# A two-layer decoder trunk on one core: every large tile at a multiple of 512 bytes with the weights' tiles 256 bytes further on, a different start, and copies of q by DMA

## The chip, the cores and the metric

The kernel runs on one core of one Trainium2 chip. The metric is the device time of one execution in microseconds (us). Before the change it is 2411.27 us, the median of three runs (2409.95 to 2413.39). Two times within about 0.2% of each other (4.8 us) can't be told apart by a measurement of this kernel.

The core has a matrix engine (TensorE; in the rows PE for its matmuls and PEld for its loads of the stationary operand), a vector engine (VectorE, DVE), a scalar engine (ScalarE, ACT), GpSimd (POOL), and a queue engine (SyncE, SP) that issues most DMAs. Each runs its own list of instructions in order, and semaphores join them.

## The reference

Input x is (1, 512, 1024) in float32: 512 positions, width 1024. Two layers follow, and a final RMSNorm. A layer is:

```python
h = rms_norm(x, norm_mix_g[i])
proj = h @ w_in[i]          # q_r,k_r,v_r,g_r | q_n,kv_n,gate_n | m_a,m_b
...
o_r = retention(qr, kr, vr)                      # 4 heads, dk 256, dv 512, rotary q and k
y_ret = (silu(g_r) * group_norm(o_r)) @ w_o_ret[i]
o_n = nsa(q_n, k_c, v_c, k_s, v_s, k_w, v_w, ...)  # 16 heads of 64, 2 key groups
y_nsa = o_n @ w_o_nsa[i]
x = x + (sigmoid(m_a) * y_ret + sigmoid(m_b) * y_nsa) @ w_out[i]
h = rms_norm(x, norm_ffn_g[i])
a, b = split(h @ w_ffn_in[i]);  x = x + (silu(a) * b) @ w_ffn_out[i]   # hidden 2816
```

The sparse attention (nsa) has three branches per head: compressed keys and values (an MLP with gelu over overlapping blocks of 32 positions, for keys and for values), selected blocks, and a window. With 512 positions all blocks are selected and the window covers everything, so the last two are full causal softmax attentions with different keys. A T5 relative bias is added to all three.

## The kernel before

**Precision and matmuls.** Every product is made of three fp32r matmuls. An operand is split into a rounded part (hi) and the rest (lo): `split` (L78) makes hi with a copy on ACT and lo with a subtraction on DVE. `mm3` (L119) then adds hi by hi, hi by lo and lo by hi into one PSUM bank (L122, L123, L124). A matmul streams its moving operand, up to 512 columns, past a stationary operand of 128 by 128 that PEld loads; the load of the next one runs while the present one streams. In the rows, `f<-hh,wh` names the output bank, the moving and the stationary operand.

**Weights.** `raw` (L86) loads up to 1 MB of a weight into a tile wr (three buffers) by one DMA on SP. `cut` (L94) splits a part of it into wh and wl (three buffers each). SP issues a load when its buffer is free, which is when the wl of an earlier user has been made.

**Two kinds of projection.** In `proj_t` (L126) the weights are stationary and the activations (hh and hl, 512 columns) move. In `proj_n` (L717), and in the values of the attention, the weights move and slices of the activations are stationary.

**Addresses.** A tile's place in SBUF follows from the sizes of all tiles allocated ahead of it, each rounded to 32 bytes: first the constants (cols, ident, rb, kcz, ...), then pool sb with the 37 slots "u" of 2 KB, ks, p, pt, gate, cv, strip, mt, ld, then the small tiles (sm), then the weights' pool wp. Before the change the slots u and the tiles p, pt and ks lie at 416 bytes past a multiple of 512, cv and strip at 160, and wr, wh and wl at 96. All slices that matmuls of 512 columns read begin at steps of 512 bytes in these tiles.

**The start.** `setup` (L133) loads constants and clears kcz. `start_x` (L232) loads x transposed in eight tiles xt (256 KB each) and the first weights, those of the compressed keys and values (1 MB), in the order two xt, the weights, six xt. `make_h` (L198) scales each xt by the norm's gain and splits it into hh and hl. The norm's other factor, rstd per position, comes later: `acc_sq` (L203) squares each xt on ACT and adds on POOL, `norm_stats` (L211) sums over partitions with small matmuls (L216) and takes the power -1/2 on POOL (L220), and `norm_bcast` (L222) spreads it: a copy rep on DVE (L225), four transposes (L229), and the tile rb on ACT (L230), by which projections are then multiplied.

**Keys and values of the attention.** `nsa_kv` (L261) makes, in this order: the two projections psc for compression (48 matmuls), the norm's sums, the key projection psk[0], rb, psk[1]. Then it steps through generators that others share: `compress` for k and v (L324; z and xa on DVE, hi and lo of xa into p or pt tiles, 32 matmuls of 256 columns at L362 in two halves, a gelu, a small projection) and `nsa_q` (L411; a projection of 24 matmuls per half quad, then qd, hi and lo, and copies of both to the other 64 partitions at L431). `keys(br)` (L272) makes the key tiles ks on DVE and ACT. The order of these steps is

```python
next(comp["k"]); fill(9)
next(comp["k"]); next(comp["k"]); next(comp["v"])
keys(0); fill(9)
next(comp["v"]); next(comp["v"]); keys(1)
```

where `fill(9)` is half a quad of q. Then come the values (96 matmuls of 304 columns), and after that 16 heads of attention, merged with the next quads' q and with gate projections.

**Who sets the order.** A scheduler puts each engine's instructions in order by the program's order and by when it expects them to be ready. `issue_after` adds an edge, so that what a block traces on one engine comes behind a given instruction there.

Of the kernel before, what the change touches and what calls it, by code (L numbers as in the profile page):

```python
# [8 lines left out]
F32 = mybir.dt.float32  # L9
F32R = mybir.dt.float32r  # L10
AF = mybir.ActivationFunctionType
ALU = mybir.AluOpType
AX = mybir.AxisListType

P = 128
T = 512
D = 1024
NT = T // P
KD = D // P
# [3 lines left out]
HN = 16  # L23
# [8 lines left out]
class Builder:  # L32
# [86 lines left out]
    def mm3(self, ps, items, start=True, stop=True):  # L119
        n = len(items)  # L120
        for i, (lh, ll, rh, rl) in enumerate(items):
            self.nc.tensor.matmul(ps, lh, rh, start=start and i == 0, stop=False)  # L122
            self.nc.tensor.matmul(ps, lh, rl, start=False, stop=False)  # L123
            self.nc.tensor.matmul(ps, ll, rh, start=False, stop=stop and i == n - 1)  # L124

    def proj_t(self, w, j, acts, bank=None):  # L126

# [5 lines left out]
    def setup(self):  # L133
        nc, a = self.nc, self.a
        self.bv = self.dr.tile([HN, 640], F32, tag="bv", name="bv")
        self.cols = self.const("cols", [P, 104])
        nc.sync.dma_start(self.cols, a["c_cols"])
        self.gmix = [self.cols[:, l * 8 : l * 8 + 8] for l in range(DEPTH)]
        self.gffn = [self.cols[:, 16 + l * 8 : 24 + l * 8] for l in range(DEPTH)]
        self.pos = {"k": [self.cols[:, 40 + l * 16 : 56 + l * 16] for l in range(DEPTH)],  # L140
                    "v": [self.cols[:, 72 + l * 16 : 88 + l * 16] for l in range(DEPTH)]}
        self.ident = self.const("ident", [P, P])
        nc.gpsimd.dma_start(self.ident, a["c_ident"])
        self.setup_bias()
        self.mhalf = self.const("mhalf", [P, NT])
        nc.vector.memset(self.mhalf, -0.5)
        self.ones = self.const("ones", [P, 1])
        nc.vector.memset(self.ones, 1.0)
        self.rb = self.const("rb", [P, T])
        self.rstd = self.const("rstd", [P, NT])  # L150
        self.hrstd = self.const("hrstd", [P, NT])
        self.kcz = [self.const(f"kcz{g}", [P, 224], F32R) for g in range(2)]
        for g in range(2):
            nc.vector.memset(self.kcz[g].bitcast(F32), 0.0)
        self.xs = self.dr.tile([KD, P, T], F32, tag="xs", name="xs")
        self.gs = self.dr.tile([2 * KD, P, T], F32, tag="gs", name="gs")
        self.gr = self.dr.tile([4 * NSPILL, P, T], F32, tag="gr", name="gr")
        self.ys = self.dr.tile([KD, P, T], F32, tag="ys", name="ys")
        self.cmask = self.const("cmask", [P, NT, 32])
        nc.gpsimd.dma_start(self.cmask, a["c_cmask"].rearrange("p (i n) -> p i n", n=32))  # L160
# [71 lines left out]
    def start_x(self):  # L232

        nc = self.nc
        xts = [self.u("xt") for _ in range(KD)]
        w = self.a["w_in"][0][:, C_KV : C_KV + 256].rearrange("(k p) n -> p k n", p=P)
        for k in range(2):
            last = nc.sync.dma_start(xts[k], self.a["c_xt"][k])
        with self.tc.issue_after(last.ins):
            raw = self.raw([(lambda v: v, w)], KD, 256)  # L240
        with self.tc.issue_after(self.last_load.ins):
            for k in range(2, KD):
                self.last_x = nc.sync.dma_start(xts[k], self.a["c_xt"][k])
        h = [self.make_h(xts[k], self.gmix[0][:, k : k + 1]) for k in range(2)]
        with self.tc.issue_after(self.last_hi.ins):
            self.first_w = [self.cut(raw[:, :, j * P : (j + 1) * P]) for j in range(2)]
        h += [self.make_h(xts[k], self.gmix[0][:, k : k + 1]) for k in range(2, KD)]
        self.first_h = self.last_hi

        def stats():  # L250
            self.bias_rows()
            acc = None
            for xt in xts:
                acc = self.acc_sq(acc, xt)
            self.norm_stats(acc)

        self.stats = stats, self.norm_bcast
        return h


    def nsa_kv(self, l, h, q0):  # L261
        nc, w = self.nc, self.a["w_in"][l]
        view = lambda c, n, k0=0, kt=KD: w[k0 * P : (k0 + kt) * P, c : c + n].rearrange("(k p) n -> p k n", p=P)
        wc = self.first_w if l == 0 else self.wcols(w, 0, KD, C_KV, 256)
        psc = [self.proj_t(wc, j, h, "f") for j in range(2)]
        with self.tc.issue_after(self.last_x.ins) if l == 0 else nullcontext():
            wk = self.raw([(lambda v: v[:, :, :P], view(C_KV + 256, P)), (lambda v: v[:, :, P:], view(C_KV + 512, P))], KD, 256)
        self.stats[0]()
        nc.vector.tensor_scalar(self.hrstd, self.rstd, 0.5, None, ALU.mult)
        ks = [self.sb.tile([P, 2, T], F32R, tag=f"ks{g}", name=self.nm("ks"), bufs=1) for g in range(2)]  # L270

        def keys(br):  # L272
            kd, kh = self.u("kd"), self.u("kh", F32R)
            nc.vector.tensor_tensor(kd, psk[br], self.rb, ALU.mult)
            lo, hi = slice(0, 64), slice(64, P)
            self.split(ks[0][lo, br], ks[0][hi, br], kd[lo])
            self.split(kh[hi], ks[1][hi, br], kd[hi])
            nc.scalar.activation(ks[1][lo, br], kd[hi], AF.Copy)

        def values(half):  # L280
            return self.chunk([(lambda v: v[:, :, 0:P], view(C_KV + 384, P, half * 4, 4)),
                               (lambda v: v[:, :, P : 256 + 48], view(C_KV + 640, P + 48, half * 4, 4))], 4, 304, "k")

        with self.tc.issue_after(self.first_h.ins) if l == 0 else nullcontext():
            wk = [self.cut(wk[:, :, br * P : (br + 1) * P]) for br in range(2)]
        psk = [self.proj_t(wk, 0, h, "a")]
        self.stats[1]()
        psk.append(self.proj_t(wk, 1, h, "a"))
        comp = {kind: self.compress(l, kind, psc[i]) for i, kind in enumerate("kv")}
        fill = lambda n: [next(q0, None) for _ in range(n)]  # L290
        next(comp["k"])
        fill(9)
        next(comp["k"])
        next(comp["k"])
        next(comp["v"])
        keys(0)
        fill(9)
        next(comp["v"])
        next(comp["v"])
        keys(1)  # L300
        vs = [self.sb.tile([P, 4, 2, 64], F32R, tag="u", name=self.nm("vs")) for _ in range(NT)]
        gate = self.sb.tile([P, NT, HN, 3], F32, tag="gate", name=self.nm("gate"), bufs=1)
        pss = [self.bank(b) for b in "aaoo"]
        for half in range(2):
            wv = values(half)
            for t in range(NT):
                ts = slice(t * P, (t + 1) * P)
                self.mm3(pss[t][:, :304], [(h[half * 4 + k][0][:, ts], h[half * 4 + k][1][:, ts], wv[k][0], wv[k][1])
                                           for k in range(4)], start=half == 0, stop=half == 1)
            if half == 0:  # L310
                for kind in "kv":
                    next(comp[kind], None)
        for t in range(NT):
            src = pss[t][:, :256].rearrange("p (b d) -> p b d", d=64)
            rc = self.rstd[:, t : t + 1]
            nc.scalar.activation(vs[t][:, :, 0, :], src, AF.Copy, scale=rc)
            nc.vector.scalar_tensor_tensor(vs[t][:, :, 1, :], src, rc, vs[t][:, :, 0, :].bitcast(F32), ALU.mult, ALU.subtract)
            gt = gate[:, t].rearrange("p h b -> p (h b)")
            nc.scalar.activation(gt, pss[t][:, 256:304], AF.Tanh, scale=self.hrstd[:, t : t + 1])
            nc.vector.tensor_scalar(gt, gt, 0.5, 0.5, ALU.mult, ALU.add)  # L320
        return ks, vs, gate
# [88 lines left out]
    def nsa_q(self, l, h, quad, qs):  # L410
# [7 lines left out]
        for a in range(2):  # L418
# [7 lines left out]
            for g in range(2):  # L426
# [1 line left out]
                r, o = (slice(x * 64, x * 64 + 64) for x in (g, 1 - g))  # L428
                self.split(hi[r], lo[r], d[r])
                for x in (hi, lo):  # L430
                    nc.scalar.activation(x[o], x[r].bitcast(F32), AF.Copy)  # L431
                qs.append((hi, lo))
            yield

# [468 lines left out]
    def last_ffn(self, l, x, h):  # L903
# [3 lines left out]
        for hf in range(2):  # L907
            gf.append(self.tile("p", NPB))
            nc.sync.dma_start(gf[hf], self.a["norm_final_g"][None, hf * 512 : hf * 512 + 512].broadcast_to([P, 512]))
        ss = self.small("ss", 2 * NT)  # L910
        base = self.small("base", NT)
        for k0, kt in GROUPS:
            hid = self.hidden(l, h, k0, kt)
# [59 lines left out]
WR = 3  # L973
WH = 3
# [4 lines left out]
AT = {"scores": (0, 0.5), "values": (0, 0.8), "finish": (0.6, 0.6), "fill": (0.1, 0.7)}  # L979
QAT = (2, 2)  # L980
NSPILL = 3
FILL = [20, 18, 8, 8, 14, 14, 8, 8, 14, 14, 8, 8, 14, 14, 14, 14, 14, 12]
BANKS = {"a": 2, "o": 2, "t": 2, "f": 2}
CYCLE = "afo"
# [65 lines left out]
```

## Time and profile before

| | |
|---|---|
| median of 3 runs | 2411.27 us |
| the profiled execution, its own time | 2411.87 us |
| its span, first to last instruction | 2409.8 us |
| granted TensorE clock, mean | 0.996 |
| PE busy | 2364.8 us (98%), 11042 matmuls |
| PEld busy | 1936.3 us (80%) |
| DVE, ACT, POOL busy | 1386.1, 1070.7, 258.2 us |
| DMA | 260 MB, mean 108 GB/s |

Busy time of PE is no measure of its speed: matmuls overlap, and the end of each is modelled, so a matmul that shows 0.39 us starts 0.23 us behind the one ahead. Where matmuls follow each other without a wait, the distance of their starts is their cost; it is read from a count in a window, or from the starts in the timeline. A wait is put down to what released it last.

### The profile page before, as it was taken

The page shows a single profiled execution, that of the slowest core. Times are in us where ns is not written, and L with a number is a line of the kernel's source. Part 1 is how long each engine was busy: PE and PEld are TensorE (multiplying, and loading weights), DVE is VectorE, ACT ScalarE, POOL GpSimd, SP SyncE. Part 2 cuts the span into 40 slices and gives each one's busy share as a digit, 9 for nine tenths or more (in the row PEclk, how much of TensorE's full clock was granted, in tenths as well). Part 3 has the DMA queues.
Part 4 walks back from the last instruction along what each step waited for, and adds up shares of the span by engine and source line. Part 5 has one row for each costly group of instructions (what it writes and reads, how often), then busy time and mean ns, then how long its engine had stood idle before and what let it go on. Part 6 is the DMA issues. An engine that isn't in the chain of part 4 may idle for free.

```text
span 2409.8 us, 29134 instructions
## 1 busy us (share of the span) xinstructions
PE 2364.8 (98%) x11042; PEld 1936.3 (80%) x11042; DVE 1386.1 (58%) x2715; ACT 1070.7 (44%) x1926; POOL 258.2 (11%) x224
## 2 busy tenths in 40 slices
PE   7999999999999999999989999999999999999998
PEld 5887778888887888888878777788888878888887
DVE  6777887354574633333577877864555754434344
ACT  5677786233333422222356777742433343322222
POOL 3000000010030110110200000001100202101010
PEclk9999999999999999999999999999999999999999
DMA  7532223522342522323444232244232533223221
GB/s 210 143 89 74 74 83 93 183 75 95 106 159 86 163 88 91 101 90 98 142 142 129 81 84 70 78 130 147 92 92 92 179 107 130 89 87 105 88 96 61
DMA packets 234172, 260.35 MB, mean 108 GB/s; under 512 B 42214, under 2 KB 178438, under 8 KB 234033
## 3 DMA queue, kind: packets, MB, share of 16 engines
q1 hardware_dynamic: 220688, 236.93, 32.3%
q10 hardware_dynamic: 13152, 21.37, 2.4%
q8 instruction: 86, 1.41, 0.2%
q14 instruction: 54, 0.43, 0.1%
q0 software_dynamic: 192, 0.21, 0.0%
HBM read 235.36 MB, written 23.11 MB: 107 GB/s over the span
## 4 chain that ended last, share of the span: by engine, by line
PE 90%; ACT 4%; DVE 4%; issue 1%; POOL 1%; DMA 0%; SPq 0%; ACTq 0%; POOLq 0%
PE f L122 12%; PE f L123 12%; PE f L124 12%; PE a L123 8%; PE a L122 8%; PE o L122 8%; PE o L123 8%; PE o L124 8%; PE a L124 8%; PE t L564 2%; PE o L556 1%; PE o L557 1%; ACT wh L79 1%; PE a L529 1%; PE a L530 1%
## 5 line engine op out<-in xcount | busy, mean ns | idle before, releaser
L79 ACT ACTIVATE wh<-wr 128x1024 fp32r<-128x1024 f32 (+3 forms) x406 | 397.9, 980 | 952.9 <-PE f L123 227.5
L80 DVE TENSOR_TENSOR wl<-wr,wh 128x1024 fp32r<-128x1024 f32 (+3 forms) x406 | 465.7, 1151 | 227.2 <-ACT wh L79 224.9
L122 PE MATMUL f<-hh,wh 128*128 128x512 f32 x936 | 373.1, 399 | 3.2 <-ACT wh L79 3.2
L123 PE MATMUL f<-hl,wh 128*128 128x512 f32 x936 | 369.9, 395 | 0.0
L124 PE MATMUL f<-hh,wl 128*128 128x512 f32 x936 | 368.1, 394 | 1.2 <-DVE wl L80 1.1
L124 PEld LDWEIGHTS f<-hh,wl 128*128 128x128 f32 x936 | 176.4, 188 | 41.9 <-DVE wl L80 3.6
L122 PEld LDWEIGHTS f<-hh,wh 128*128 128x128 f32 x936 | 176.4, 188 | 37.7 <-ACT wh L79 5.0
L123 PEld LDWEIGHTS f<-hl,wh 128*128 128x128 f32 x936 | 176.6, 189 | 30.7
L511 ACT ACTIVATE p<-p,nmx 128x512 f32<-128x512 f32 (+3 forms) x256 | 142.5, 557 | 53.7 <-DVE nmx L510 51.2
L80 DVE TENSOR_TENSOR pt<-t,pt 128x512 fp32r<-128x512 f32 (+3 forms) x256 | 123.2, 484 | 50.6 <-ACT pt L79 49.3
L874 POOL TENSOR_TENSOR fa<-fa,rb 128x512 f32<-128x512 f32 x44 | 77.6, 1763 | 562.2 <-ACT fa L873 562.2
L510 DVE CUSTOM_DVE_ANT_0 p<-a,strip 128x512 f32<-128x512 f32 (+3 forms) x256 | 119.4, 483 | 25.2 <-PE a L530 15.6
L123 PE MATMUL a<-hl,wh 128*128 128x512 f32 x336 | 132.4, 394 | 0.0
L122 PE MATMUL a<-hh,wh 128*128 128x512 f32 x336 | 132.4, 394 | 0.0
L124 PE MATMUL a<-hh,wl 128*128 128x512 f32 x336 | 131.2, 390 | 0.0
L79 ACT ACTIVATE pt<-t 128x512 fp32r<-128x512 f32 (+3 forms) x256 | 109.1, 427 | 47.6 <-PE t L564 43.5
L123 PE MATMUL o<-hl,wh 128*128 128x512 f32 x328 | 129.2, 394 | 0.0
L122 PE MATMUL o<-hh,wh 128*128 128x512 f32 x328 | 129.0, 393 | 0.0
L124 PE MATMUL o<-hh,wl 128*128 128x512 f32 x328 | 127.9, 390 | 0.0
L564 PE MATMUL t<-ident,p 128*128 128x128 f32 x640 | 113.9, 273 | 0.0
L564 PEld LDWEIGHTS t<-ident,p 128*128 128x128 f32 x640 | 81.2, 140 | 23.6 <-DVE pt L80 1.7
L556 PE MATMUL o<-pt,vs 128*128 128x512 f32 (+3 forms) x256 | 92.8, 365 | 3.2 <-ACT pt L79 3.2
(405 smaller groups left out, 4842.7 us busy)
## 6 DMA issues: line engine op xcount, KB each, us to landing
wr<-in_w_in SPq DMA_DIRECT2D x66, 1024.0 KB, 5.3
wr<-in_w_ffn_in SPq DMA_DIRECT2D x44, 1024.0 KB, 5.1
wr<-in_w_ffn_out SPq DMA_DIRECT2D x18, 1024.0 KB, 5.0
wr<-in_w_o_ret SPq DMA_DIRECT2D x16, 1024.0 KB, 5.0
wr<-in_w_in SPq DMA_DIRECT2D x36, 256.0 KB, 4.6
strip<-bv SPq DMA_DIRECT2D x32, 256.0 KB, 4.0
gs<-mt ACTq DMA_DIRECT2D x32, 256.0 KB, 2.0
wr<-in_w_o_nsa SPq DMA_DIRECT2D x16, 512.0 KB, 6.5
```

The lines of the kernel that those rows point to most:

```text
L79: self.nc.scalar.activation(hi, src, AF.Copy)
L80: (eng or self.nc.vector).tensor_sub(lo, src, hi.bitcast(F32))
L122: self.nc.tensor.matmul(ps, lh, rh, start=start and i == 0, stop=False)
L123: self.nc.tensor.matmul(ps, lh, rl, start=False, stop=False)
L124: self.nc.tensor.matmul(ps, ll, rh, start=False, stop=stop and i == n - 1)
L510: nc.vector.tensor_tensor_reduce(p, src, self.backwards(strip, w - 1, w), -1.0, BIG, ALU.add, ALU.min, nmx[:, c])
L511: nc.scalar.activation(p, p, AF.Exp, scale=-1.0, bias=nmx[:, c], accum_out=sm[:, c])
L529: nc.tensor.matmul(ps[:, :w], qh[:, ts], ks[:, br, :w], start=True, stop=False)
L530: nc.tensor.matmul(ps[:, :w], ql[:, ts], ks[:, br, :w], start=False, stop=True)
L556: nc.tensor.matmul(po[:, j * P :], lhs, th, start=br == 0 and j == 0, stop=False)
L564: nc.tensor.transpose(pt[:, (i - j) * P : (i - j + 1) * P], pr[br][i][:, j * P : (j + 1) * P], self.ident)
L874: nc.gpsimd.tensor_mul(t, t, self.rb)
```

## The change

- Two unused tiles, pad in the constants (96 bytes) and pad among the small tiles (448 bytes), gate widened from 192 to 256 columns, and ss with two buffers instead of six. With these the slots u, p, pt, ks, cv and strip begin at multiples of 512 bytes, and wr, wh and wl 256 bytes past one.
- In setup an activation on hrstd, and 32 matmuls of 224 columns on the cleared kcz, whose result nobody reads.
- `start_x` loads weights in four pieces of 256 KB, each ahead of a pair of xt, and cuts and splits them pair by pair. The first two projections go through k in the outer loop and through the two columns of tiles in the inner one.
- In layer 0 the squares are added on DVE instead of POOL, the sums come behind psk[0] and rb behind the first half of psk[1]; `bias_rows` comes after the statistics. In layer 1 the sums come between the two psc and rb behind them. hrstd is made behind all of that.
- The first step of the values' compression comes ahead of the third of the keys', and keys(0) comes behind the values' last matmuls.
- The copies at L431 (64 of 64 by 512) become DMAs issued on SP.

```diff
-            self.nc.tensor.matmul(ps, ll, rh, start=False, stop=stop and i == n - 1)
+            self.last_mm = self.nc.tensor.matmul(ps, ll, rh, start=False, stop=stop and i == n - 1)
...
+        self.const("pad", [P, 24])
...
+        self.small("pad", PAD, bufs=1)
...
+        nc.scalar.activation(self.hrstd, self.mhalf, AF.Copy)
...
+        ps = self.tp()
+        for _ in range(IDLE):
+            nc.tensor.matmul(ps[:, :224], self.kcz[0][:, :P], self.kcz[1], start=True, stop=True)
...
-        xts = [self.u("xt") for _ in range(KD)]
         w = self.a["w_in"][0][:, C_KV : C_KV + 256].rearrange("(k p) n -> p k n", p=P)
-        for k in range(2):
-            last = nc.sync.dma_start(xts[k], self.a["c_xt"][k])
-        with self.tc.issue_after(last.ins):
-            raw = self.raw([(lambda v: v, w)], KD, 256)
-        with self.tc.issue_after(self.last_load.ins):
-            for k in range(2, KD):
+        raw = self.wp.tile([P, 2048], F32, tag="wr", name=self.nm("wr"), bufs=WR).rearrange("p (k n) -> p k n", k=KD)
+        xts, h, self.first_w, order = [], [], [], nullcontext
+        for k in range(KD):
+            with order():
+                if k % 2 == 0:
+                    nc.sync.dma_start(raw[:, k : k + 2], w[:, k : k + 2])
+                xts.append(self.u("xt"))
                 self.last_x = nc.sync.dma_start(xts[k], self.a["c_xt"][k])
-        h = [self.make_h(xts[k], self.gmix[0][:, k : k + 1]) for k in range(2)]
-        with self.tc.issue_after(self.last_hi.ins):
-            self.first_w = [self.cut(raw[:, :, j * P : (j + 1) * P]) for j in range(2)]
-        h += [self.make_h(xts[k], self.gmix[0][:, k : k + 1]) for k in range(2, KD)]
+            order = lambda: self.tc.issue_after(self.last_x.ins)
+        for k in range(0, KD, 2):
+            if k % 4 == 0:
+                hi, lo = (self.wp.tile([P, 1024], F32R, tag=t, name=self.nm(t), bufs=WH).rearrange("p (k n) -> p k n", k=4)
+                          for t in ("wh", "wl"))
+            with self.tc.issue_after(self.last_hi.ins) if k else nullcontext():
+                self.split(hi[:, k % 4 : k % 4 + 2], lo[:, k % 4 : k % 4 + 2], raw[:, k : k + 2])
+            self.first_w += [(hi[:, k % 4 + i], lo[:, k % 4 + i]) for i in range(2)]
+            h += [self.make_h(xts[k + i], self.gmix[0][:, k + i : k + i + 1]) for i in range(2)]
...
         def stats():
-            self.bias_rows()
             acc = None
             for xt in xts:
-                acc = self.acc_sq(acc, xt)
+                sq = self.u("sq")
+                nc.scalar.activation(sq, xt, AF.Square)
+                if acc is not None:
+                    nc.vector.tensor_add(sq, acc, sq)
+                acc = sq
             self.norm_stats(acc)
+            self.bias_rows()
...
-        wc = self.first_w if l == 0 else self.wcols(w, 0, KD, C_KV, 256)
-        psc = [self.proj_t(wc, j, h, "f") for j in range(2)]
+        if l == 0:
+            psc = [self.bank("f") for _ in range(2)]
+            for k in range(KD):
+                for j in range(2):
+                    wh, wl = (v[:, j * P : (j + 1) * P] for v in self.first_w[k])
+                    self.mm3(psc[j], [(wh, wl, *h[k])], start=k == 0, stop=k == KD - 1)
+        else:
+            wc = self.wcols(w, 0, KD, C_KV, 256)
+            psc = [self.proj_t(wc, 0, h, "f")]
+            self.stats[0]()
+            psc.append(self.proj_t(wc, 1, h, "f"))
+            self.stats[1]()
...
-        self.stats[0]()
-        nc.vector.tensor_scalar(self.hrstd, self.rstd, 0.5, None, ALU.mult)
...
         psk = [self.proj_t(wk, 0, h, "a")]
-        self.stats[1]()
-        psk.append(self.proj_t(wk, 1, h, "a"))
+        if l == 0:
+            with self.tc.issue_after(self.last_mm.ins):
+                self.stats[0]()
+        psk.append(self.bank("a"))
+        for half in range(2):
+            part = range(4 * half, 4 * half + 4)
+            self.mm3(psk[1], [(wk[1][0][:, k], wk[1][1][:, k], *h[k]) for k in part], start=half == 0, stop=half == 1)
+            if l == 0 and half == 0:
+                with self.tc.issue_after(self.last_mm.ins):
+                    self.stats[1]()
+        nc.vector.tensor_scalar(self.hrstd, self.rstd, 0.5, None, ALU.mult)
...
         next(comp["k"])
         fill(9)
         next(comp["k"])
+        next(comp["v"])
         next(comp["k"])
-        next(comp["v"])
-        keys(0)
         fill(9)
         next(comp["v"])
         next(comp["v"])
+        keys(0)
         keys(1)
...
-        gate = self.sb.tile([P, NT, HN, 3], F32, tag="gate", name=self.nm("gate"), bufs=1)
+        gate = self.tile("gate", 1, w=256)[:, : NT * HN * 3].rearrange("p (t h b) -> p t h b", t=NT, h=HN)
...
                 for x in (hi, lo):
-                    nc.scalar.activation(x[o], x[r].bitcast(F32), AF.Copy)
+                    nc.sync.dma_start(x[o].bitcast(F32), x[r].bitcast(F32))
...
-        ss = self.small("ss", 2 * NT)
+        ss = self.small("ss", 2 * NT, bufs=2)
...
+PAD = 112
+IDLE = 32
```

## Rows read from the trace of the kernel before

**Rows 1.** Waits of TensorE: who waited for whom, us in total, times, longest.
```profile
PE o L362 <- DVE pt L80: 6.2, 2, 3.1
PE o L362 <- DVE wl L80: 6.1, 6, 2.5
```

**Rows 2.** Timeline of the start: us, duration, engine, line, operation, idle before and releaser.
```profile
1.01 0.48 DVE L154 MEMSET kcz<- 128x224 f32 x2
...
2.12 0.43 SPq L91 DMA_DIRECT2D wr<-in_w_in  x1
...
4.10 1.28 ACT L83 ACT_TABLE_LOAD   x1 [4.10 <-DMA xt<-c_xt]
...
10.73 2.00 ACT L79 ACTIVATE wh<-wr 128x1024 fp32r<-128x1024 f32 x2 [4.00 <-DMA wr<-in_w_in]
...
11.84 0.80 PE L122 MATMUL f<-hh,wh 128*128 128x512 f32 x1 [2.55 <-ACT wh L79]
...
16.06 0.40 PE L122 MATMUL f<-hh,wh 128*128 128x512 f32 x1
...
25.16 0.40 PE L122 MATMUL a<-hh,wh 128*128 128x512 f32 x1
```

**Rows 3.** Windows: us, busy time (count) by engine, PEclk, DMA share, GB/s.
```profile
5.00:10.00 5.00, 1.00 (x2) 0.13 (x2) 1.41 (x2) 1.72 (x3) 0.00 (x0) 1.00 1.03 358
```

**Rows 4.** Norm of layer 0: timeline, and all rep copies (ns, min/median/max).
```profile
19.85 11.49 POOL L208 TENSOR_TENSOR sq<-sq,sq 128x512 f32<-128x512 f32 x7
...
33.19 1.04 POOL L220 TENSOR_TENSOR rstd<-var,mhalf 128x4 f32<-128x4 f32 x1 [1.86 <-DVE var L219]
34.20 2.07 POOL L344 MEMSET xa<- 128x256 f32 x8
...
36.61 0.66 PE L229 MATMUL t<-ident,rep 128*128 128x128 f32 x4 [1.80 <-DVE rep L225]
...
L225 DVE COPY rep<-rstd x4: 427/1318/2210, 34.3 to 2043.9; 128x512 f32<-128x512 f32 x4
```

**Rows 5.** Stretch behind the keys: windows (both layers), the chain, DVE's timeline, line L431.
```profile
37.90:72.80 34.90, 28.12 (x141) 23.83 (x140) 30.10 (x57) 24.25 (x39) 0.00 (x0) 0.85 0.41 123
1224.00:1258.00 34.00, 26.80 (x133) 22.16 (x132) 28.06 (x54) 23.09 (x36) 0.00 (x0) 0.90 0.33 96
...
47.99 0.44 ACT qh L431
...
51.53 0.52 ACT ql L431
...
59.77 0.69 DVE L274 TENSOR_TENSOR kd<-a,rb 128x512 f32<-128x512 f32 x1
...
L431 ACT ACTIVATE qh<-qh x32: 628/630/637, 48.0 to 1511.2; 64x512 fp32r<-64x512 f32 x32
```

**Rows 6.** SP's own waits, and DMA issues (count, KB each, median us to landing).
```profile
SPq L91 <- DVE wl L80: 1430.6, 165, 21.1
...
gs<-mt ACTq DMA_DIRECT2D x32, 256.0 KB, 2.0
```

**Rows 7.** Windows of three projections, and the timeline of a product inside the retention.
```profile
900.00:1000.00 100.00, 100.00 (x439) 82.06 (x438) 38.52 (x42) 25.06 (x30) 9.05 (x5) 1.00 0.30 95
2130.00:2165.00 35.00, 35.00 (x152) 28.05 (x151) 11.32 (x12) 6.36 (x6) 0.00 (x0) 1.00 0.28 91
2180.00:2250.00 70.00, 70.00 (x302) 56.71 (x301) 28.62 (x33) 20.79 (x26) 10.83 (x6) 1.00 0.28 97
...
587.60 0.39 PE L122 MATMUL f<-p,pt 128*128 128x512 f32 x1
...
592.36 0.39 PE L122 MATMUL a<-hh,wh 128*128 128x512 f32 x1
```

**Rows 8.** Groups of matmuls by line and form: count, busy us, mean ns, idle before.
```profile
L122 PE MATMUL f<-hh,wh 128*128 128x512 f32 x936 | 373.1, 399 | 3.2 <-ACT wh L79 3.2
...
L122 PE MATMUL o<-wh,hh 128*128 128x512 f32 x128 | 50.7, 396 | 0.0
```

## The prediction

> **What bounds the kernel now.** I read the page first, then the waits of TensorE, then the stretches. Its long waits lie in two places: the first 40 us, and the stretch after the keys' projections in each layer, where L362 waits 6.2 us for DVE's pt and 6.1 us for DVE's wl [rows 1]. Everywhere else the time is the number of matmuls times their spacing. So the change can act in three ways: at the start, in those two stretches, and, by the addresses of the tiles, on the spacing of every matmul. I work on the profiled execution: span 2409.8 us, its own time 2411.9, and the median of the runs is 0.6 under that.
>
> **The start.** Now: the whole weight tile of 1 MB is issued at 2.12 us, ACT first loads its table (1.28 us), the split waits for the weights until 10.73, the first real matmul is at 11.84, it and the eight behind it come 0.47 us apart at the slow clock until 16.06, and the second projection begins (a<-hh) at 25.16 [rows 2]. After: weights come in four pieces of 256 KB between the x tiles, the table load is pulled ahead by the activation on hrstd, and 32 matmuls of 224 columns on zeros run from the end of the kcz memset (1.49 us) [rows 2].
> - DMA. The first x landed by 4.1 us, when the table load starts [rows 2]; the first piece (issued where x was) should land then and x a little later. Eight x tiles and 1 MB are 3.1 MB; from 5 to 10 us the DMA moved 358 GB/s [rows 3], so with 310 GB/s for these pieces, the constants taking the rest, a pair of k (0.79 MB) lands every 2.5 us: 5.5, 8.0, 10.6, 13.1.
> - TensorE. 0.47 us for 512 columns at the slow clock are 0.2 us for 224. The clock rose 4.2 us after the first real matmul; counted from 1.5 that is 5.7, by then 21 of the 32 are done, the other eleven take 0.1 each: 6.8 us. From there 12 matmuls a pair at 0.23 are 2.8 us, slower than the DMA's 2.5, so PE sets it: 6.8 + 48 x 0.229 = 17.8 us, against 25.16 (0.229 from [rows 7]). With a slip for the splits (1.5 us behind each landing) I take **7 us** saved, between 5 (DMA at 250 GB/s) and 8.5. What is late next is the keys' weights, issued behind the last x: another 1 MB, 3.3 us after 13.1, and about 2 us for its split, 18.4. That is the slip.
>
> **The norm.** Now POOL adds the squares until 31.3, and the broadcast copy rep takes 2.21 us where its shortest is 0.43, beside POOL's memsets of xa; L229 starts at 36.61 [rows 4]. After, DVE adds, ahead of need, and the second half of psk[1] (12 matmuls, 2.8 us) covers most of the chain var, pow (rstd, 1.04 us) and rep (0.43 to 2.21). The loss there is about 2.8 us now (L229's wait of 1.8, the rest an estimate for the small matmuls, which stay). I take **1.5 us** saved, 0.5 to 2.2. In layer 1 the statistics move one projection earlier, behind and before a projection each as now; I count nothing.
>
> **The stretch after the keys, twice.** [...] The change takes keys(0) (kd 0.69 and two ks of 0.69, 2.1 us of DVE) behind the last cut that TensorE waits for, puts the z and xa of the values ahead of the second half of the keys' compression, and takes the copies of qh and ql (0.63 us each on ACT, four per half) out of ACT, where four of them stand between 47.99 and 52.0 in the chain that ends last [rows 5]. So the first wait (3.1 us for pt, each layer) goes, since pt no longer starts at TensorE's last q matmul; of the second (half of 6.1) perhaps half stays, since DVE's total work in the stretch is the same. Lost now: 6.2 + 6.1 us of waits and, by the clock, at most 0.15 x 34.9 + 0.10 x 34.0 = 8.6 us, together 20.9. I take **13 us** for both layers: 6.2 of the first waits, 3 of the second, 4 of the clock. Low end 6 (the first waits alone), high end 19. What is late next is keys(0) and keys(1): they now sit beside the values' 96 matmuls of 304 columns (by columns 0.136 us each, 13 us), which cover their 4.1 us of DVE.
>
> **The q copies.** There are 64 (two rows of 32), 40 us of ACT [rows 5], but outside the two stretches TensorE's long waits name none of them, so I count no gain there. They become 64 DMAs of 128 KB on SP. The nearest landing is 2.0 us for 256 KB [rows 6], against 2.5 us of ACT for the same four; I take **1 us** lost in all, from 1 gained to 10 lost.
>
> **The layout.** The two pads, gate's 256 columns and the smaller ss move every large tile. With all slots rounded to 32 bytes and laid out in the order of allocation, u, p, pt and ks tiles go from 416 to 0 past a multiple of 512, the weights' from 96 to 256. What the trace shows of it [rows 7]: weights stationary, activations moving: 439 matmuls (two of them reach in from before) in 100 us, 0.2288 us each. Weights moving: 150 in 35 us, 0.2333. Both operands at 416 (p,pt): 21 from 587.60 to 592.36, 0.2267. So the spacing is not one number, and pairs at different offsets differ by up to 3%. But the first kind also ran at 0.2333 for 70 us (300 matmuls), at the same addresses, so part of it is a state and not the address. The first kind has 3 x 2288 = 6864 matmuls (fifteen groups, the largest 936), the second 3 x 496 = 1488 (six groups, the largest 128) [rows 8]. The new distance from moving to stationary, 256, lies midway between the first kind's 192 and the second's 320; no row has it. Bounds: everything at 0.2267 gives 6864 x 2.1 + 1488 x 6.6 ns = 24 us gained; the first kind at 0.2333 gives 6864 x 4.5 = 31 us lost. I take **0**, the nearest row being the first kind's own.
>
> [...]
>
> **Sum.** 7 + 1.5 + 13 - 1 + 0 = 20.5 us: 2411.9 - 20.5 = 2391.4, less 0.6 for the median: 2391 us, with 2381 to 2401 as this case's own range (start and norm 5.5 to 10.7, stretches 6 to 19, not all at one end).
>
> **Rivals.**
> - Layout gains too: all spacings at 0.2267. 2391 - 24 = 2367. For it: the pair at equal offsets, and 256 is half a period, so it could behave like 0. Against it: the pair with a row has a distance of 0, not of 256.
> - Layout costs, the slower side: the first kind takes the 0.2333 that weights-moving pairs show. 2391 + 31 = 2422 at the full price, 2406 halfway. For it: the distance moves toward 320, and the first kind has shown that state. It decides from 3.0 ns a matmul on (20.5 us over 6864), where the other gains are used up.
> - SP's queue: the q DMAs wait for the split, in order, on the queue that loads the weights. SP waits for wl 165 times, 8.7 us in the mean [rows 6]; if each of the six later quads finds its copies behind one such wait, the first matmuls on q start 8.7 us late: 52 us, 2443. It decides once a copy stands behind a load that waits longer than the way to the first use. Against it: the split and the weights' release both follow TensorE's order, so the queue meets them in about the order in which they come.
>
> **How the numbers follow.** Forecast 0.40 (all of it faster). Layout gains 0.24 (faster). Layout costs 0.26: a third of it near 2406 or below, 0.08 faster, 0.07 same, 0.11 slower. SP's queue 0.10: partial stalls at most, 0.05 faster, 0.02 same, 0.03 slower. Together faster 0.77, same 0.09, slower 0.14; 0.2% (4.8 us) is about what a measurement of this kernel can tell from no change. For 8 in 10 the range goes from 2362 to 2421: beyond lie some 0.06 of the layout's gain and 0.12 of its cost and of SP.
>
> **What would show it.** The first a<-hh matmul near 18 us instead of 25.16; L229 close behind half of psk[1]; no wait of L362 for pt, and PEclk near 1.00 in the stretch after the keys of both layers; in the long projections 437 matmuls per 100 us if the layout does nothing, 441 if it gains, 429 if it costs. The prediction is wrong if that count moves by more than 2, or if waits for DMA appear before L441.

## The result and the profile after

The changed kernel takes 2383.15 us (median of 4 runs, 2383.07 to 2385.5); the kernel before, measured beside it, 2411.82. The ratio is 0.9881, 95% interval 0.9869 to 0.9893: 28.7 us faster, where 20.5 were forecast. 2383 lies 8 us under the predicted 2391 and inside the range. But that the sum came out near is luck: one term of 13 us brought nothing, and one of 0 brought 23. Without the layout, the steps that were forecast at 20.5 us brought 3.4.

The profiled execution went from a span of 2409.8 to 2383.7 us (after, it is the longest of the four, 2385.5 us by its own time). Its 26.1 us by stage, from the starts of the first matmul of each stage in the two traces (after less before): up to the second projection -7.0; from there to q -1.8; q to the values, layer 0, -0.3; values +0.3; the rest of the heads +1.5; retention -3.9; the mix of both -0.3; feed-forward -3.5. Layer 1: sums to values +0.1; values +0.9; heads +0.5; retention -5.3; mix -0.3; feed-forward -7.0.

**The start and the norm.** TensorE's timeline after, to be held against [rows 2, 4] (us, duration, engine, line, operation, in brackets idle time before and releaser; line numbers have moved, L229 is now L236):

```profile
1.53 5.94 PE L161 MATMUL t<-kcz,kcz 128*128 128x224 f32 x32 [1.53 <-DVE kcz L157]
7.31 0.41 PE L122 MATMUL f<-hh,wh 128*128 128x512 f32 x1
7.55 0.39 PE L123 MATMUL f<-hl,wh 128*128 128x512 f32 x1
...
18.20 0.39 PE L122 MATMUL a<-hh,wh 128*128 128x512 f32 x1
...
27.91 0.60 PE L236 MATMUL t<-ident,rep 128*128 128x128 f32 x4
```

The first real matmul comes at 7.31 instead of 11.84, its successors 0.23 us apart at once, and the second projection at 18.20 instead of 25.16. The transposes of the norm stand directly behind the first half of psk[1], without the 1.80 us of idle time of before.

**The stretch after the keys.** Its windows after, to be held against [rows 5] (us, busy time and count of PE, PEld, DVE, ACT, POOL, PEclk, DMA share, GB/s), and then TensorE's waits over the whole run, against [rows 1] (who for whom, us in total, times, longest; L362 is now L395):

```profile
37.90:72.80 34.90, 27.37 (x161) 23.80 (x160) 28.37 (x50) 20.24 (x35) 0.53 (x1) 0.85 0.67 193
1224.00:1258.00 34.00, 26.90 (x153) 23.64 (x154) 27.09 (x52) 18.52 (x34) 0.53 (x1) 0.85 0.63 175
```

```profile
PE f L124 <- DVE wl L80: 6.1, 2, 3.1
PE o L395 <- DVE pt L80: 5.8, 2, 3.0
...
PE f L474 <- DMA qh<-qh: 2.0, 2, 1.1
PE f L475 <- DMA ql<-ql: 1.8, 2, 1.0
```

Nothing that was to go is gone: a wait for pt of 3 us in each layer, one for wl of 3 us in each layer, and a granted clock of 0.85. What is new is the place. The timelines of TensorE and, in the second fence, DVE, same columns as above:

```profile
41.66 0.39 PE L122 MATMUL f<-hh,wh 128*128 128x512 f32 x1
41.89 0.40 PE L123 MATMUL f<-hl,wh 128*128 128x512 f32 x1
45.31 0.58 PE L395 MATMUL o<-wh,pt 128*128 128x256 f32 x1 [3.02 <-DVE pt L80]
48.95 0.80 PE L124 MATMUL f<-hh,wl 128*128 128x512 f32 x1 [3.06 <-DVE wl L80]
49.54 0.63 PE L122 MATMUL f<-hh,wh 128*128 128x512 f32 x1
49.97 0.63 PE L123 MATMUL f<-hl,wh 128*128 128x512 f32 x1
```

```profile
41.42 1.75 DVE L370 TENSOR_TENSOR z<-f,rb 64x256 f32<-64x256 f32 x4
43.19 1.51 DVE L381 TENSOR_TENSOR xa<-z,cols 128x124 f32<-128x124 f32 x5
44.83 0.76 DVE L80 TENSOR_TENSOR pt<-xa,pt 128x256 fp32r<-128x256 f32 x2
...
47.68 1.21 DVE L80 TENSOR_TENSOR wl<-wr,wh 128x1024 fp32r<-128x1024 f32 x1
...
56.51 0.69 DVE L458 SCALAR_TENSOR_TENSOR qd<-f,rb 128x512 f32<-128x512 f32 x1 [4.67 <-PE f L124]
```

TensorE does two matmuls of q's second half, and then has one product on pt next in its order: it waits 3.02 us for it. The third matmul of q needs a wl that DVE makes only at 47.68, behind z, xa and the lo parts of pt. So q's second half, which has nothing to do with pt, stands behind it, starts over 0.43 us apart (the granted clock reads 0.50 from 48.95 to 53.40), ends at 56.3, and DVE sits idle for 4.67 us waiting for it before it can make qd.

**The long projections.** The windows of [rows 7] after, of TensorE alone (us, busy time and count, PEclk, DMA share, GB/s):

```profile
900.00:1000.00 100.00, 100.00 (x443) 1.00 0.29 95
2130.00:2165.00 35.00, 35.00 (x156) 1.00 0.33 110
2180.00:2250.00 70.00, 70.00 (x310) 1.00 0.27 93
```

The counts were 439, 152 and 302. Less the two that reach in, 441 in 100 us are 0.2268 us each, where 437 were 0.2288; and both kinds of projection now run at about 0.227. This is the number that the prediction gave for "the layout gains", and a count that moves by more than 2 was one of its two signs of being wrong.

### The profile page after: what moved, and what is told of

Read it like the earlier page. It is cut to its first block, busy times and chain, and to the rows that moved or that the text cites. A ratio compares the mean times of both kernels' runs of the same rounds, so it can differ in the third digit from the quotient of the medians.

```text
span 2383.7 us, 29325 instructions
## 1 busy us (share of the span) xinstructions
PE 2345.6 (98%) x11074; PEld 1941.3 (81%) x11074; DVE 1378.7 (58%) x2724; ACT 1034.8 (43%) x1865; POOL 249.5 (10%) x217
## 4 chain that ended last, share of the span: by engine, by line
PE 93%; DVE 3%; DMA 2%; ACT 1%; POOL 1%; issue 1%; POOLq 0%; ACTq 0%; DVEq 0%
PE f L122 12%; PE f L124 12%; PE f L123 12%; PE o L122 7%; PE a L123 7%; PE o L123 7%; PE o L124 7%; PE a L122 7%; PE a L124 7%; PE t L597 3%; PE o L590 2%; PE o L589 2%; PE a L562 1%; PE a L563 1%; DMA wr<-in_cmp_w_v 1%
## 5 line engine op out<-in xcount | busy, mean ns | idle before, releaser
L79 ACT ACTIVATE wh<-wr 128x1024 fp32r<-128x1024 f32 (+2 forms) x408 | 398.6, 978 | 934.8 <-PE f L123 236.4
L80 DVE TENSOR_TENSOR wl<-wr,wh 128x1024 fp32r<-128x1024 f32 (+2 forms) x408 | 462.8, 1138 | 206.8 <-ACT wh L79 203.8
L124 PE MATMUL f<-hh,wl 128*128 128x512 f32 x936 | 369.2, 395 | 6.1 <-DVE wl L80 6.1
L123 PE MATMUL f<-hl,wh 128*128 128x512 f32 x936 | 369.0, 394 | 0.0
L124 PEld LDWEIGHTS f<-hh,wl 128*128 128x128 f32 x936 | 177.1, 189 | 44.2 <-DVE wl L80 6.7
L123 PEld LDWEIGHTS f<-hl,wh 128*128 128x128 f32 x936 | 177.3, 189 | 30.2
L79 ACT ACTIVATE pt<-t 128x512 fp32r<-128x512 f32 (+3 forms) x256 | 109.7, 431 | 59.8 <-PE t L597 57.4
L124 PE MATMUL a<-hh,wl 128*128 128x512 f32 x336 | 130.8, 389 | 0.0
L123 PE MATMUL a<-hl,wh 128*128 128x512 f32 x336 | 130.7, 389 | 0.0
L124 PE MATMUL o<-hh,wl 128*128 128x512 f32 x328 | 127.6, 389 | 0.0
L123 PE MATMUL o<-hl,wh 128*128 128x512 f32 x328 | 127.6, 389 | 0.0
```

The lines of the kernel that those rows point to most:

```text
L79: self.nc.scalar.activation(hi, src, AF.Copy)
L80: (eng or self.nc.vector).tensor_sub(lo, src, hi.bitcast(F32))
L124: self.last_mm = self.nc.tensor.matmul(ps, ll, rh, start=False, stop=stop and i == n - 1)
```

## The experiments

Ratios are to the kernel before, run beside each on the same chip. Theory D: the layout's gain hangs on the distance between the addresses of the moving and the stationary operand, modulo 512 bytes. B: on the alignment of the tiles by itself. S: it is a state that follows from the new start. For the stretch, Q: the order of DVE's work and of TensorE's; W: DVE's total work.

**The layout alone.** On the kernel before:

```diff
+        self.const("pad", [P, 24])
+        self.small("pad", PAD, bufs=1)
-        gate = self.sb.tile([P, NT, HN, 3], ...)
+        gate = self.tile("gate", 1, w=256)...
-        ss = self.small("ss", 2 * NT)
+        ss = self.small("ss", 2 * NT, bufs=2)
+PAD = 112
```

Expected: 

> The kernel before with the layout of the change and nothing else (both pads, gate of 256 columns, ss with two buffers). Theory L (most of the 26 to 29 us is the layout, through the spacing of the 512-column matmuls, which fell from 0.2288 and 0.2333 to 0.2267 us in the trace after): 2391 to 2395 us, that is 17 to 21 us under the kernel before, 441 matmuls per 100 us in the long projections, and the start and the stretch behind the keys as before (first a<-hh at 25 us). Rival S (the spacing is a state that the new start brings about, not the addresses): 2408 to 2414 us, spacing 0.2288 and 0.2333 as before.

Measured: 2388.19 us, ratio 0.9904 (0.9890 to 0.9919), 23.0 us faster than before's 2411.23, and more than the 17 to 21 us of theory L. The start is the old one, so S falls. Its first window:

```profile
900.00:1000.00 100.00, 100.00 (x443) 1.00 0.31 102
```

**All but the layout.** The changed kernel with those lines undone.

Expected: 

> The changed kernel without the layout (no pads, gate of 192 columns, ss with six buffers, so that u, p, pt and ks lie at 416 and the weights at 96 past a multiple of 512, as before); start, norm, order of the keys and q copies as changed. Theory L: 2402 to 2406 us, 6 to 10 us under the kernel before (7 of the start, 1.8 of the norm, nothing of the stretch behind the keys, 1 to 2 lost in the attention), spacing 0.2288 and 0.2333 again. Rival S: 2383 to 2388, spacing 0.2267.

Measured: 2407.80 us, ratio 0.9984 (0.9974 to 0.9993): 3.4 us, less than the 6 to 10 of theory L. Start, norm, order and q copies together bring 3.4, though the first matmuls of q come 7.5 us earlier in its trace (32.3 against 39.8). Most of that is lost again behind it: in layer 0 q to the values takes 0.7 us longer than before, the heads take 1.7 and 1.5 us longer in the two layers, the values 0.3 and 1.0. Its windows are those of before; here the first and the last:

```profile
900.00:1000.00 100.00, 100.00 (x439) 1.00 0.29 95
2180.00:2250.00 70.00, 70.00 (x301) 1.00 0.29 91
```

The two parts give 23.0 + 3.4 = 26.4 of the 28.0 us that their kernel before (2411.23) stands over 2383.2.

**Everything 32 bytes further.** `self.const("pad", [P, 32])` in place of 24: tiles at 32 and 288, distance 256 as in the changed kernel, multiples of 512 no more.

Expected: 

> The changed kernel with the first pad 32 bytes larger, so that every tile behind it lies 32 bytes further on: u, p, pt and ks at 32, the weights at 288 past a multiple of 512. The distance between the operands is the 256 of the change; what is gone is that tiles begin at a multiple of 64 bytes. Theory D (the distance between moving and stationary operand, modulo 512, sets the spacing): 2381 to 2386 us, spacing 0.2267. Theory B (what counts is that each operand begins at a multiple of 64 bytes or more): 2398 to 2406 us, spacing 0.2288 or more.

Measured: 2383.69 us, ratio 0.9887 (0.9872 to 0.9901). "Every large tile at a multiple of 512" is not what counts; B falls.

**Distance 192.** `PAD = 96`: the large tiles stay at multiples of 512, the weights go from 256 to 192 past one.

Expected: 

> The changed kernel with the second pad 64 bytes smaller: u, p, pt and ks at multiples of 512, the weights 192 bytes past one. The distance from moving activations to stationary weights is the 192 of the kernel before, but every tile begins at a multiple of 64 bytes. Theory D (distance): 2396 to 2406 us, spacing 0.2288 with weights stationary and 0.2333 with weights moving. Theory B (alignment): 2381 to 2386 us, spacing 0.2267 in both kinds.

Measured: 2407.78 us, ratio 0.9984 (0.9974 to 0.9994). 64 bytes on the weights' side cost 24 us, with the same start and the same order, 2 us more than the range of theory D. Its windows, the last two moved to the same stage (2 us earlier), and below them the groups of one output bank between 900 and 1000 us (count, busy us, mean ns, idle before), with a group of the changed kernel in the same window, and one of this kernel's last window, behind them:

```profile
900.00:1000.00 100.00, 100.00 (x439) 1.00 0.29 95
2128.00:2163.00 35.00, 35.00 (x152) 1.00 0.28 90
2178.00:2248.00 70.00, 70.00 (x307) 1.00 0.30 100
```

```profile
L123 PE MATMUL o<-hl,wh 128*128 128x512 f32 x32 | 12.6, 394 | 0.0
L122 PE MATMUL o<-hh,wh 128*128 128x512 f32 x32 | 12.5, 392 | 0.0
L124 PE MATMUL o<-hh,wl 128*128 128x512 f32 x32 | 12.4, 388 | 0.0
...
L124 PE MATMUL o<-hh,wl 128*128 128x512 f32 x36 | 14.0, 389 | 0.0
...
L124 PE MATMUL a<-hh,wl 128*128 128x512 f32 x37 | 14.6, 394 | 0.0
```

In the changed kernel all three groups show 389 ns. At 192 the three matmuls of a group are unequal, and not by their operands: hh by wl is the one that is not slower between 900 and 1000 us (388), and the slowest in the last window (394, with 388 for hh by wh). So the distance sets the mean of the three, and not what a given pair of tiles costs. In the last window 306 matmuls of this kernel start between 2177.98 and 2248.02 us, 0.2289 us each.

**Distance 0.** `PAD = 48`: the weights' tiles at multiples of 512 too.

Expected: 

> The changed kernel with every large tile, the weights' too, at a multiple of 512 bytes (distance 0 between moving and stationary operand, where the change has 256). If the spacing hangs on the distance and 0 is as good as 256, as the pair p,pt at equal offsets suggests (0.2267 us a matmul): 2383 us, within 3. If 0 is worse than 256 for two operands in one bank or row: the projections' 6864 + 1488 matmuls at 0.2288 and 0.2333 again, 2407 us. If 256 is itself not the best and 0 goes lower, to 0.224 say: 8352 x 2.7 ns = 22 us less, 2361.

Measured: 2383.94 us, ratio 0.9891 (0.9876 to 0.9905), 443, 156 and 310 in the three windows. 0 and 256 are the same, and below 0.2267 nothing was seen.

**Distance 320.** `PAD = 128`: the weights at 320, so that each kind of projection has the distance that the other had before.

Expected: 

> The changed kernel with the weights' tiles at 320 past a multiple of 512 and the large tiles at 0: the projections with weights stationary get the distance that weights-moving ones had before (320, 0.2333 us) and the other way round (192, 0.2288). If the spacing is a function of the signed distance: 6864 x 6.6 ns and 1488 x 2.1 ns more than at 256, 48 us: 2431. If only the size of the distance counts (320 is 192 the other way): as at 192, 2408. If weights moving were slow by themselves: 1488 at 0.2333 and the rest at 0.2288, 2383 + 10 + 14 = 2407.

Measured: 2423.55 us, ratio 1.0053 (1.0038 to 1.0068), 40 us slower than the changed kernel. Windows, the second at the same stage as above, and one of the three groups (L123 and L124 show 394 too):

```profile
900.00:1000.00 100.00, 100.00 (x431) 1.00 0.29 95
2142.00:2177.00 35.00, 35.00 (x154) 1.00 0.28 90
```

```profile
L122 PE MATMUL o<-hh,wh 128*128 128x512 f32 x32 | 12.6, 394 | 0.0
```

In the second window the weights move, and the distance is now 192. A count in 35 us is too coarse here; these two starts lie 153 matmuls apart:

```profile
2142.02 0.39 PE L122 MATMUL a<-wh,fh 128*128 128x512 f32 x1
...
2177.04 0.39 PE L122 MATMUL o<-wh,fh 128*128 128x512 f32 x1
```

Weights stationary, 429 in 100 us are 0.2331, close to the 0.2333 that weights-moving pairs showed before at this distance; weights moving, 35.02 us by 153 are 0.2289, what weights-stationary pairs showed before at 192. So the distance has a sign, and which tile holds the weights doesn't matter. The price, 40 us, is below the forecast 48: the heads, where projections of q stand among matmuls of other shapes, take 330.5 and 330.7 us here and 330.2 and 329.1 in the changed kernel, so there the spacing shows little.

**q's copies back on ScalarE.** In the changed kernel:

```diff
-  nc.sync.dma_start(x[o].bitcast(F32), x[r].bitcast(F32))
+  nc.scalar.activation(x[o], x[r].bitcast(F32), AF.Copy)
```

Expected: 

> The changed kernel with the copies of q's halves back on ScalarE (64 of 0.63 us) in place of the DMAs. Theory A, the copies as DMAs cost only the waits that the trace shows (3.8 us at the first products of the heads): these go, 2379 us. Theory B, the copies come back into the chain of the stretch after the keys and DVE or ACT is late with the values' operands: 2.5 us in each layer, 2388. If neither, 2383 within 2.

Measured: 2376.93 us, ratio 0.9861 (0.9847 to 0.9876), past both theories. The heads are 1.8 and 0.5 us shorter than in the changed kernel, since the waits of L474 and L475 are gone. But the stretch is shorter too, 25.9 instead of 28.6 us in layer 0 and 2.9 us less in layer 1: with the copies elsewhere the scheduler wrote TensorE's order otherwise. The first product on pt now comes behind all 24 matmuls of q's second half, where the changed kernel had it behind two of them:

```profile
48.44 0.39 PE L124 MATMUL f<-hh,wl 128*128 128x512 f32 x1
48.67 0.28 PE L395 MATMUL o<-wh,pt 128*128 128x256 f32 x1
```

and so the longest of TensorE's waits between 25 and 80 us is now this, the 3 us ones are gone:

```profile
PE o L395 <- DVE wl L80: 3.5, 4, 1.4
```

**The values' first step later.** In the changed kernel, the copies still by DMA:

```diff
         next(comp["k"])
-        next(comp["v"])
         next(comp["k"])
+        next(comp["v"])
         fill(9)
```

Expected: 

> The changed kernel with the first step of the values' compression (z and xa on DVE) moved back behind the third step of the keys' compression, the keys' products still late. Theory Q (the stretch won nothing because v's z and xa now stand on DVE ahead of the cuts of q's second half, so that TensorE waits 3.0 us twice a layer and its clock falls): the waits for wl and pt of 6.1 and 5.8 us shrink to half or less, and the stretch from q's first to the values' first matmul is 24 to 26 us instead of 28.6: 2373 to 2379. Theory W (DVE's total work sets the stretch, whatever the order): the waits only move, 2383 within 2. As before the change: the pt wait comes back behind q, 2383 to 2386.

Measured: 2377.74 us, ratio 0.9865 (0.9849 to 0.9882). From q to the values it is 25.0 us instead of 28.6, and in layer 1 3.8 us less, as theory Q had it. The window, and the longest waits of TensorE between 25 and 80 us:

```profile
37.90:72.80 34.90, 30.05 (x187) 26.92 (x187) 31.70 (x60) 22.91 (x42) 0.53 (x1) 0.95 0.72 220
```

```profile
PE o L395 <- DVE wl L80: 3.7, 4, 2.5
PE o L395 <- DVE pt L80: 0.5, 1, 0.5
```

DVE does more in the same 34.9 us (31.70 instead of 28.37), and the granted clock is 0.95 instead of 0.85.

**Both.**

Expected: 

> The changed kernel with both edits: q's copies on ScalarE and the values' first step behind the keys' third. Alone they gave 2376.9 and 2377.7, from 2383.2. If the two gains are one and the same (both let TensorE take q's second half ahead of the first product on pt): 2376 to 2377. If the heads' part of the copies (waits for DMA, 3.8 us by the trace of after) comes on top of the order's 5.4: 2374. If they added in full: 2371.5.

Measured: 2380.43 us, ratio 0.9877 (0.9860 to 0.9893), under neither alone, and none of the three cases. The totals lie within 0.2% of each other, but the traces agree with them: q to the values takes, in both layers together, 57.4 us in the changed kernel, 51.8 and 50.0 with either edit alone, and 54.7 with both. The wait for pt is back at 3.1 us a layer. DVE's timeline shows what precedes pt:

```profile
44.64 1.23 DVE L80 TENSOR_TENSOR wl<-wr,wh 128x1024 fp32r<-128x1024 f32 x1 [0.67 <-ACT wh L79]
...
48.45 2.36 DVE L381 TENSOR_TENSOR xa<-z,cols 128x124 f32<-128x124 f32 x8
50.85 0.69 DVE L458 SCALAR_TENSOR_TENSOR qd<-f,rb 128x512 f32<-128x512 f32 x1
51.45 1.42 DVE L80 TENSOR_TENSOR pt<-xa,pt 128x256 fp32r<-128x256 f32 x4
```

All eight xa and qd stand ahead of the first lo part of pt, and the xa begin late: DVE waited for a wh that stands on ACT behind two copies of q (41.97 to 43.11 us). With the copies by DMA and the values' first step later, xa began at 46.52, and the first two pt stood behind five xa, at 48.32. So of the 3.1 us some 1.9 are the later begin, which the copies on ACT go with, and 1.2 the order on DVE:

```profile
46.52 0.38 DVE L381 TENSOR_TENSOR xa<-z,cols 128x124 f32<-128x124 f32 x1
...
47.16 1.26 DVE L381 TENSOR_TENSOR xa<-z,cols 128x124 f32<-128x124 f32 x4
48.32 0.77 DVE L80 TENSOR_TENSOR pt<-xa,pt 128x256 fp32r<-128x256 f32 x2
```

**Both, and xa on GpSimd.** `(nc.gpsimd if kind == "v" else nc.vector).tensor_tensor(xv...)`.

Expected: 

> The kernel with both edits, and the values' eight additions that make xa (0.38 us each by DVE's rows) moved from DVE to GpSimd. If DVE's total work in the stretch sets it, 2 to 3 us a layer come off DVE before the cuts of the second half of q and of the values: 4 to 6 us under the kernel with both edits, 2368 to 2371. If the additions on GpSimd take long and pt waits for them instead: slower than it by 2 to 6 us.

Measured: 2380.04 us, ratio 0.9875 (0.9860 to 0.9890): no difference from "both", which neither theory has. Eight additions take GpSimd 4.73 us where DVE needed 2.36, and the wait for pt stays (3.0 us).

**Both, and keys(0) early.** keys(0) back ahead of the second `fill(9)`.

Expected: 

> The kernel with both edits, but the products keys(0) back ahead of q's second half, as before the change. If moving the keys late is worth what it takes off DVE there (2.1 us a layer, the step of the forecast): 4 us slower than the kernel with both edits, 2378 to 2380. If it only moves work within the stretch: the same within 2.

Measured: 2380.85 us, ratio 0.9878 (0.9864 to 0.9893): 0.4 us from "both", which is nothing. So in the total, moving the keys late brings nothing here. It mostly moves work: with the keys early q to the values takes 1.3 and 1.6 us longer (28.8 in each layer), and in layer 0 the next stage, from the values' first matmul to the first of the heads, takes 1.3 us less (16.4 instead of 17.7).

**No matmuls on zeros.** `IDLE = 0`.

Expected: 

> The changed kernel without the 32 matmuls on zeros at the start. Theory C, they bring the clock up before the first real matmul and are worth that: without them the first real matmul stays at 7.3 us, it and the next ones run 0.47 us apart for some 4.2 us as before the change, and what is lost is 9 x 0.24 = 2 us at most, less what the DMA hides: second projection of the keys at 18.5 to 20.5 instead of 18.2, total 2383 to 2386. Theory S, DMA alone sets the start: no difference, 18.2.

Measured: 2385.42 us, ratio 0.9895 (0.9880 to 0.9910). The total can't tell it from the changed kernel, but the trace can:

```profile
6.15 0.80 PE L122 MATMUL f<-hh,wh 128*128 128x512 f32 x1 [6.15 <-ACT hh L83]
...
11.37 0.63 PE L124 MATMUL f<-hh,wl 128*128 128x512 f32 x1
11.80 0.57 PE L122 MATMUL f<-hh,wh 128*128 128x512 f32 x1
...
20.19 0.39 PE L122 MATMUL a<-hh,wh 128*128 128x512 f32 x1
```

The first real matmul could start at 6.15, 1.2 us before the 32 on zeros let it; it and its successors then run 0.43 us apart, the first two 0.79 and 0.59, until 11.80, and the second projection begins at 20.19 instead of 18.20. By these two traces the matmuls on zeros are worth 2.0 of the start's 7.0 us. That is rough: in the profiles of the eleven kernels with this start and the zeros, the second projection begins between 17.83 and 19.46.

## Why the forecast was right in sum and wrong in its parts

- **The start, 7 us:** right, 7.0 (5.7 to 7.3 by the other kernels with this start), and without the slip for the splits. About 2 of it are the wide spacing that the matmuls on zeros take away (0.43 us until 11.80 without them). That this is a slow clock, as the prediction has it, the granted clock doesn't show: before, it reads 1.00 from 11.84 to 16.06, while nine matmuls take 4.22 us. What speaks for it is that the same spacing stands at a reading of 0.50 behind the waits of 3 us.
- **The norm, 1.5 us:** right, 1.8. rep took 0.40 us, and half of psk[1] covers the chain.
- **The stretch after the keys, 13 us:** this step failed; measured 0.3 in layer 0 and -0.1 in layer 1. It read right that the wait for pt and the clock are what can be won (the mended order wins 3.6 and 3.8 us): the 0.15 and 0.10 in its sum are what PEclk lacks of 1.00 in the two windows of [rows 5], and before, behind the wait of 3.09 us, it reads 0.50 from 60.85 to 70.30. It failed where it said that the first wait goes, "since pt no longer starts at TensorE's last q matmul": it looked at when DVE starts pt, not at what that puts back on DVE (the wl of q's second half, behind z, xa and pt) nor at where the scheduler would then put the first product on pt. One product in the wrong place held up 22 matmuls of q. It also priced keys(0) as work that leaves the chain; the run with the keys early shows no such price in the total.
- **The q copies, 1 us lost:** mis-sized. As DMAs they land 2.9 and 3.1 us after their issue (median of 32 each), not 2.0. The row that it took for them, 2.0 us, is of ACT's queue; the same view of before had one of SP's queue, which the copies use, at 3.1 (below, columns as in [rows 6], and a line of after). The waits of the heads on them (L474 and L475) are 3.8 us, which the prediction had named as the other sign of being wrong. Taken back, 6.3 us go. By the two traces, whose executions differ by 8.2 us, the heads are 2.3 shorter and the two stretches 5.6, with some 0.6 lost at the values: most came not through the wait but with TensorE's order, which the sum didn't count.

```profile
ga<-gs SPq DMA_DIRECT2D x32, 256.0 KB, 3.1
...
qh<-qh SPq DMA_DIRECT2D x32, 128.0 KB, 2.9
```

- **The layout, 0:** this step failed, and it decides the sum. It took the first kind's own 0.2288 because it was the nearest row. The rival with every spacing at 0.2267 had the price right (24 us; 23.0 alone) and the condition too (256 behaves like 0), though no run shows that 512 bytes is the period. The rival with 0.2333 for the first kind had a real price, but of another distance: its 429 matmuls in 100 us are what 320 gives, and 256 costs nothing although it lies on the way there. 64 bytes of distance, from 256 to 192, are 24 us, at a granted clock of 1.00 in the long rows and with nothing else changed.
- **The rival of SP's queue:** not seen; the heads lost 2 us, not 52.

What stays open: how the distance gets into the spacing. The mean time of a weight load between 900 and 1000 us is 187 to 188 ns before, after, and at the distances 192 and 320, so it doesn't show there. Nor is the distance everything at 192: the last window, weights stationary, had 302 and 301 in 70 us (0.2333) before and without the layout, but 307 (0.2289) in the kernel with the weights at 192. A pad also moves the weights' tiles for ACT, DVE and the DMAs that write them; that the two operands of TensorE are what counts is argued from the same spacing in rows with different work beside them, and was not tested apart. And that the one product on pt, ordered ahead of q, is what held the stretch rests on two edits that each put it back, and each also moved other work; its place alone was not changed, nor is it known why the scheduler chose it.

## What to carry to other kernels

Where matmuls follow each other without a wait, compare their spacing between pairs of tiles: one that is 1 to 3% over the shortest row (here 0.2288 and 0.2333 us over 0.2267) may hang on where the two operands lie to each other, and a pad moves it. Count what a moved step puts ahead of the work that others wait for, engine by engine, and look up where the first instruction that needs it then stands; a gain that is read from a wait's length is only there if nothing takes its place. Two edits that each win by a better order need not add up, since each makes the order anew: either one alone (2376.9 and 2377.7 us) has a lower median than both together (2380.4).

## What the runs showed of the hardware

In long rows of fp32r matmuls of 512 columns at a granted clock of 1.00, the spacing followed the address of the stationary operand less that of the moving one, modulo 512 bytes: 0.2267 us at 0 and 256, 0.2288 at 192 (0.2333 in one stretch of the kernels before and without the layout), 0.2331 at 320. At 192 it is a mean over three unequal matmuls (388, 392 and 394 ns busy), and which of the three is the slow one changes from stretch to stretch (hl by wh between 900 and 1000 us, hh by wl in the last window). Moving all tiles by 32 bytes changes nothing (443 matmuls in 100 us, two of them reaching in, as in the changed kernel). Other distances weren't run, and these four can't tell a period of 512 bytes from one of 256.
